# Where three adds and eight bias loads are issued: VectorE adds the gate's squares, ScalarE issues the attention's bias tiles

## The chip, the cores and the metric

The kernel runs on one core of one Trainium2 chip. The metric is the device time of an execution in microseconds (us). Engines are named as in the profile: PE is TensorE's matmul stream and PEld its weight loads, DVE is VectorE, ACT is ScalarE, POOL is GpSimd, SP is SyncE, which here only issues DMAs.

## The reference, cut to what matters

One step of a one-layer hybrid decoder, for a prompt of 512 tokens and for 8 samples of 4 new tokens each, with the same weights (all in fp32):

```
x += 0.5 * SwiGLU_1(RMSNorm(x))
h  = RMSNorm(x);  [q|k|v|u] = h @ W_in
x += concat(RMSNorm(DilatedAttn(q,k,v)), RMSNorm(S5_GLU(u))) @ W_out
x += 0.5 * SwiGLU_2(RMSNorm(x))
x += sigmoid(RMSNorm(x) @ W_gate) * (p @ W_ple);  final RMSNorm
```

DilatedAttn has 8 heads of 64 and three branches, (window 128, dilation 1), (512, 4) and (2048, 16), with a relative-position bias; the branches are merged by their log-sums. The samples attend to a cache of 2048 positions per sample, and the cache, shifted by four tokens, is an output as well. S5_GLU is a state-space scan, then `out = z * sigmoid(z @ w_glu + b_glu)` with z a GELU. The two places of the change lie in the RMSNorm of `out` (its sum of squares over 512 features) and in the prompt's bias, which is added to its scores.

## The kernel before, in words

Activations lie with features on the 128 partitions and all 544 tokens (512 prompt, 32 sample) along the free dimension. Every large weight is read from memory as a 128x512 `raw` tile, cast by ACT to a high part (`whi`, L175), and DVE subtracts to get the low part (`wlo`, L176); PE then does three matmuls per tile pair (L194). SP issues these weight loads from three `raw` buffers, and the large cache copies as well.

There are three stages. The first is the first feed-forward block (with the setup of the S5 tables beside it), until about 470 us. The second, mixed stage, holds the projections, the S5 half, the sample attention, the prompt attention and most of the output projection, until about 770 us. The third is the second feed-forward block and the gated embedding. In the first and the third stage the order of the instructions of PE, DVE, ACT and POOL is set by a planner at compile time, by its own timeline; SP's order is as written. In the mixed stage all five engines run in the order in which the Python code emits them, and that is written out by hand: `ORDER` is a list of step names, and every name advances one generator by one step (`do`, with what must have come before it in `need`).

The steps that matter here:

- `glu(m)`, four tiles. ACT makes the sigmoid, DVE multiplies (L1220), and `ssm_st.add(sg)` adds up the squares: the first call squares into the accumulator (L251), each later call has ACT square into a temporary tile (L254) and an adder engine add it (L255). Adders come from the list that `Stat` was made with. Then `split_gain` has ACT make `xh` (L299) and DVE `xl` (L300). The finished sum is read by PE at L263.
- `att_q`, 16 units of prompt scores (four head pairs of four row blocks). For each unit PE makes the scores (L1014), DVE adds the bias tile `bt` and takes the minimum (L1020), ACT takes the exponential (L1022) and scales by the reciprocal of the sum (L1025). `load_bt(hp)` loads the two bias tiles of a head pair, 128x512 each, from a table in memory; it is called once ahead of unit 0 and then at the end of the last unit of a head pair (units 3, 7, 11), for the next one. The tiles share a pool of eight slots with `L`, `pt`, `kb1` and `kt1`.
- `sample_scores` (names SQ) loads `kk` and `qb` through POOL's queue and multiplies them on DVE (L1099, L1100).
- `sample_out(gr)`, for two groups of four samples: nine accumulation steps on PE (L1191), each with a pair of V-cache tiles `vv` of 512 KB, which POOL issues one step ahead (L1178). `vv` shares six slots with `pz` (one per group) and with the tiles of the S5 half.

POOL's queue in the mixed stage thus holds, in the written order: loads of `kk`, `qb`, `kb1`, `bt` and `vv`, one store of `qD`, and the three adds of the GLU tiles.

Of the kernel before, what the change touches and what calls it, by code (L numbers as in the profile page):

```python
# [18 lines left out]
P = 128  # L19
# [9 lines left out]
DA = 512  # L29
# [73 lines left out]
def decoder_step(ctx: ExitStack, tc: tile.TileContext, a: dict, o: list):  # L103
    nc = tc.nc
    V, A, PE, SP, Q = nc.vector, nc.scalar, nc.tensor, nc.sync, nc.gpsimd

    def dram(t, off, dims):
        return bass.AP(tensor=t.tensor, offset=t.offset + off, ap=dims)
# [6 lines left out]
    def sb(pool, shape, name, dt=F32, **kw):  # L115
        return pool.tile(shape, dt, name=name, **kw)

    qD = dpool.tile([NS, DA], F32, name="qD")
    btD = dpool.tile([NH, P, 641], F32, name="btD")
# [622 lines left out]
    with ExitStack() as st:  # L742
# [255 lines left out]
        bts, Ls, pts = {}, {}, {}  # L998

        def load_bt(hp):  # L1000
            for e in range(2):
                bts[hp, e] = s5([P, 512], "bt")
                Q.dma_start(bts[hp, e], dram(btD, (2 * hp + e) * P * 641 + 127, [[640, P], [1, 512]]))

        def att_q():
            load_bt(0)
            yield
            for u, (hp, i) in enumerate(units):
                w = (i + 1) * P
                pss, mns = [], []  # L1010
                for e in range(2):
                    pr = slice(64 * e, 64 * e + 64)
                    ps = psm()
                    PE.matmul(ps[:, :w], qT[pr, hp, i * P:(i + 1) * P], kT[pr, hp, 0:w], start=True, stop=True)  # L1014
                    pss.append(ps)
                for e in range(2):
                    Ls[u, e] = L = s5([P, 512], "L")
                    mn = sb(small, [P, 4], "mn", bufs=4)
                    mns.append(mn)
                    V.tensor_tensor_reduce(L[:, :w], pss[e][:, :w], bts[hp, e][:, 512 - w:], -1.0, 3e38, ALU.add,  # L1020
                                           ALU.min, mn[:, 0:1])
                    A.activation(L[:, :w], L[:, :w], AF.Exp, scale=-1.0, bias=mn[:, 0:1], accum_out=mn[:, 1:2])  # L1022
                for e in range(2):
                    V.reciprocal(mns[e][:, 2:3], mns[e][:, 1:2])
                    A.activation(Ls[u, e][:, :w], Ls[u, e][:, :w], AF.Copy, scale=mns[e][:, 2:3])  # L1025
                if i == 3 and hp < 3:
                    load_bt(hp + 1)
                yield
# [174 lines left out]
            V.tensor_copy(att[:, :, S + 16 * gr:S + 16 * gr + 16], pf)  # L1203
            yield

        ssm_st, att_st = Stat(DA, (Q,)), Stat(DA)
        att_st.accs.append(sb(small, [P, NT], "sacc", bufs=2))
        att_sq = att_st.accs[0][:, :S]
        rs = {1: ssm_st, 0: att_st}
# [247 lines left out]
def run_tile(nc, args, outs):  # L1457
    with tile.TileContext(nc, schedule_with_timeline_sim=TS) as tc:
        with tc.manual_schedule(engines=ENG):
            decoder_step(tc, args, outs)  # L1460
# [18 lines left out]
```

## Time and profile before

| | |
|---|---|
| median of 3 runs | 1298.36 us (1295.39 to 1302.9) |
| the profiled execution | 1290.02 us, its span 1288.2 us |
| granted clock of PE, mean | 0.968 |
| PE matmul / PEld busy | 1208.3 us (94%) / 1142.4 us (89%) |
| DVE / ACT / POOL busy | 713.5 us (55%) / 446.1 us (35%) / 121.8 us (9%) |
| DMA | 231.30 MB, 180 GB/s in the mean |

How to read it: shares are of the span. An engine executes its instructions in order; a row of a timeline gives the start in us from the start of the span, the duration in us, the engine, the line, the operation with its tiles (output first) and, in brackets, how long the engine had been idle just before and what ended that. Instructions of one engine overlap a little, so a next start can lie before the end of the one ahead. PE's busy time is modelled, and a granted clock of 1.00 is TensorE's upper level.

### The profile page before, as it was taken

Reading aid. Unit: us, or ns where it says so; the run is one execution under the profiler, and the core shown is the slowest. Engines: PE = TensorE matmul, PEld = TensorE weight load, DVE = VectorE, ACT = ScalarE, POOL = GpSimd, SP = SyncE. Lnnn points to the kernel's source line nnn. Section 1 sums busy time; section 2 is a strip of 40 time slices with the busy share of each in tenths; the row PEclk is TensorE's granted clock in tenths of the full one; section 3 lists DMA queues with packets and bytes.
Section 4 is the critical chain, followed back from the end, with each engine's and each line's share of the span. In section 5 each row is a group of like instructions: output and inputs, shape, how many; then the busy total and the mean of one; then the engine's idle time right before and its main releaser. Section 6 shows DMA issues by size and latency. Waiting matters only on the chain.

```text
span 1288.2 us, 23223 instructions
## 1 busy us (share of the span) xinstructions
PE 1208.3 (94%) x9518; PEld 1142.4 (89%) x9518; DVE 713.5 (55%) x1499; ACT 446.1 (35%) x889; POOL 121.8 (9%) x195
## 2 busy tenths in 40 slices
PE   8999999999999999994769889999999999999995
PEld 7899999999999988983645449999999999999994
DVE  5544478476447638777775548444433444444455
ACT  5333322322233323121754445333322223333344
POOL 2200000233000112110123311000000000000000
PEclk8999999999999998996979989999999999999998
DMA  8484566668546549766358855445566455222321
GB/s 248 134 260 147 173 217 226 227 198 258 191 167 207 170 138 299 233 203 218 91 207 243 255 172 191 155 144 199 174 217 231 153 192 180 80 83 77 93 64 70
DMA packets 207547, 231.30 MB, mean 180 GB/s; under 512 B 8647, under 2 KB 187735, under 8 KB 206416
## 3 DMA queue, kind: packets, MB, share of 16 engines
q1 hardware_dynamic: 189552, 170.35, 40.8%
q0 software_dynamic: 17856, 59.45, 14.3%
q8 instruction: 75, 1.23, 0.4%
q14 instruction: 32, 0.26, 0.1%
q10 hardware_dynamic: 32, 0.01, 0.0%
HBM read 217.46 MB, written 81.89 MB: 232 GB/s over the span
## 4 chain that ended last, share of the span: by engine, by line
PE 81%; DMA 6%; DVE 5%; issue 4%; ACT 3%; POOL 1%; SPq 0%; ACTq 0%; POOLq 0%; DVEq 0%
PE acc L194 72%; DMA vv<-in_cache_v_dram 2%; DMA raw<-in_w_in_dram 1%; PE acc L206 1%; PE acc L1441 1%; DVE kk L1099 1%; DMA raw<-in_ffn_w_up_dram 1%; DMA pc<-pD 1%; PE sm L915 1%; PE po L1191 1%; DMA mm<-mD 1%; PE sm L910 1%; PE sm L263 1%; POOL vv L1178 1%; ACT L L1022 1%
## 5 line engine op out<-in xcount | busy, mean ns | idle before, releaser
L194 PE MATMUL acc<-xh,whi 128*128 128x272 f32 x1888 | 398.5, 292 | 5.9 <-DVE qT L773 1.3
L194 PE MATMUL acc<-xl,whi 128*128 128x272 f32 x1888 | 393.9, 290 | 0.7 <-DVE xl L304 0.3
L194 PE MATMUL acc<-xh,wlo 128*128 128x272 f32 x1888 | 393.4, 289 | 0.9 <-DVE wlo L176 0.9
L175 ACT CAST whi<-raw 128x512 fp32r<-128x512 f32 (+2 forms) x348 | 208.3, 606 | 531.1 <-PE acc L194 462.0
L176 DVE TENSOR_TENSOR wlo<-raw,whi 128x512 fp32r<-128x512 f32 (+2 forms) x348 | 231.1, 671 | 200.7 <-ACT whi L175 198.2
L194 PEld LDWEIGHTS acc<-xh,whi 128*128 128x128 f32 x1888 | 297.4, 189 | 12.0 <-issue 4.0
L194 PEld LDWEIGHTS acc<-xl,whi 128*128 128x128 f32 x1888 | 299.0, 190 | 1.9 <-DVE xl L304 0.8
L194 PEld LDWEIGHTS acc<-xh,wlo 128*128 128x128 f32 x1888 | 297.7, 189 | 1.4 <-DVE wlo L176 1.3
L194 PE MATMUL acc<-hh,whi 128*128 128x272 f32 x704 | 145.7, 288 | 0.0
L194 PE MATMUL acc<-hh,wlo 128*128 128x272 f32 x704 | 145.3, 288 | 0.0
L194 PE MATMUL acc<-hl,whi 128*128 128x272 f32 x704 | 145.2, 288 | 0.0
L194 PEld LDWEIGHTS acc<-hh,whi 128*128 128x128 f32 x704 | 110.7, 188 | 0.0
L194 PEld LDWEIGHTS acc<-hh,wlo 128*128 128x128 f32 x704 | 110.7, 188 | 0.0
L194 PEld LDWEIGHTS acc<-hl,whi 128*128 128x128 f32 x704 | 110.5, 188 | 0.0
L362 DVE TENSOR_TENSOR s<-acc,rstd 128x544 f32<-128x544 f32 x44 | 31.9, 724 | 87.3 <-PE acc L194 87.3
L356 DVE TENSOR_TENSOR s<-acc,rstd 128x544 f32<-128x544 f32 x44 | 31.9, 724 | 72.1 <-PE acc L194 65.9
L303 ACT CAST hh<-s 128x544 fp32r<-128x544 f32 x44 | 28.5, 647 | 78.9 <-DVE s L363 78.9
L304 DVE TENSOR_TENSOR hl<-s,hh 128x544 fp32r<-128x544 f32 x44 | 31.9, 725 | 27.3 <-ACT hh L303 27.3
L370 DVE SCALAR_TENSOR_TENSOR x<-acc,x 128x544 f32<-128x544 f32 x32 | 23.2, 725 | 36.0 <-PE acc L194 36.0
L1099 DVE TENSOR_TENSOR kk<-kk,qb 128x1024 f32<-128x1024 f32 x32 | 38.9, 1217 | 5.6 <-DMA qb<-qD 5.6
L1100 DVE TENSOR_REDUCE sc<-kk 128x16 f32<-128x1024 f32 x32 | 39.0, 1220 | 1.1
L357 ACT ACTIVATE s<-s 128x544 f32<-128x544 f32 x44 | 29.0, 659 | 11.5 <-DVE s L356 11.2
(397 smaller groups left out, 1116.6 us busy)
## 6 DMA issues: line engine op xcount, KB each, us to landing
out_dram<-in_cache_k_dram SPq DMA_DIRECT2D x32, 1022.0 KB, 7.0
out_dram<-in_cache_v_dram SPq DMA_DIRECT2D x32, 1022.0 KB, 6.0
raw<-in_ffn_w_gate_dram SPq DMA_DIRECT2D x44, 512.0 KB, 4.0
raw<-in_ffn_w_up_dram SPq DMA_DIRECT2D x44, 512.0 KB, 4.0
vv<-in_cache_v_dram POOLq DMA_DIRECT2D x36, 512.0 KB, 6.4
raw<-in_ffn_w_down_dram SPq DMA_DIRECT2D x32, 512.0 KB, 3.8
kk<-in_cache_k_dram POOLq DMA_DIRECT2D x32, 512.0 KB, 5.8
raw<-in_w_in_dram SPq DMA_DIRECT2D x16, 512.0 KB, 8.8
```

Source lines behind the costliest of these rows:

```text
L175: A.copy(hi[:, :len(p), :], r)
L176: V.tensor_tensor(lo[:, :len(p), :], r, hi[:, :len(p), :].bitcast(F32), ALU.subtract)
L194: PE.matmul(ps[:, h, :HT], wt[:, j, :], z[:, h * HT:(h + 1) * HT], start=done == 0 and n == 0, stop=done == len(ks) - 1 and n == 2)
L206: PE.matmul(ps[:, h, :HT], wt[:, j, :], z[:, h * HT:(h + 1) * HT], start=hf == 0 and j == 0 and n == 0, stop=hf == 1 and j == 3 and n == 2)
L303: A.copy(hi, src)
L304: V.tensor_tensor(lo, src, hi.bitcast(F32), ALU.subtract)
L356: V.tensor_tensor(v2(g1), pg[:, :, :HT], v2(rstd()), ALU.mult)
L357: A.activation(g1, g1, AF.Silu)
L362: V.tensor_tensor(v2(u1), pu[:, :, :HT], v2(rstd()), ALU.mult)
L370: V.scalar_tensor_tensor(v2(x[:, m, :]), ps[:, :, :HT], 0.5, v2(x[:, m, :]), ALU.mult, ALU.add)
L1099: V.tensor_tensor(t_, t_, qbs[n // 2], ALU.mult)
L1100: V.tensor_reduce(scs[b // 4][:, f, b % 4, 16 * jp:16 * jp + 16], t_.rearrange("p f (h d) -> p (f h) d", d=HD), AX.X, ALU.add)
```

## The change

Two lines. `Stat` is made without a list of adders for the gate's statistics, and its default is DVE alone; and the bias loads are issued from ACT's queue in place of POOL's.

```diff
         def load_bt(hp):
             for e in range(2):
                 bts[hp, e] = s5([P, 512], "bt")
-                Q.dma_start(bts[hp, e], dram(btD, (2 * hp + e) * P * 641 + 127, [[640, P], [1, 512]]))
+                A.dma_start(bts[hp, e], dram(btD, (2 * hp + e) * P * 641 + 127, [[640, P], [1, 512]]))
...
-        ssm_st, att_st = Stat(DA, (Q,)), Stat(DA)
+        ssm_st, att_st = Stat(DA), Stat(DA)
```

`Q` is POOL, `A` is ACT, `V` is DVE. The places of both in the written order stay the same. POOL keeps its part of the sums of the first norm and of the norm ahead of the second feed-forward block (`Stat(D, (Q, V))`).

## Rows read from the trace of the kernel before

**Rows 1.** The page's chain of waits: shares of the span by engine.
```profile
PE 81%; DMA 6%; DVE 5%; issue 4%; ACT 3%; POOL 1%; SPq 0%; ACTq 0%; POOLq 0%; DVEq 0%
```
**Rows 2.** Windows: length; busy of PE, PEld, DVE, ACT, POOL; PEclk; DMA share; GB/s.
```profile
640.00:690.00 50.00, 37.61 (x274) 28.04 (x275) 38.39 (x98) 30.06 (x73) 12.54 (x21) 0.83 0.60 195
690.00:725.00 35.00, 30.78 (x217) 16.91 (x217) 19.16 (x46) 13.44 (x35) 10.76 (x16) 1.00 0.90 265
...
880.00:1200.00 320.00, 320.00 (x2553) 319.81 (x2553) 134.20 (x205) 96.02 (x158) 0.00 (x0) 1.00 0.47 155
```
**Rows 3.** PE's waits, 640 to 690, then 690 to 775: us, times, longest.
```profile
PE pw L965 <- DVE mn L1020: 7.1, 2, 7.0
...
PE po L1191 <- DMA vv<-in_cache_v_dram: 6.1, 4, 2.7
```
**Rows 4.** Line 255, all its DVE instructions: ns min/median/max, first and last start.
```profile
L255 DVE TENSOR_TENSOR sacc<-sacc,s x20: 707/725/1874, 23.0 to 1203.2; 128x544 f32<-128x544 f32 x20
```
**Rows 5.** Line 300, its four instructions on s (the GLU tiles).
```profile
L300 DVE SCALAR_TENSOR_TENSOR xl<-s,gains,xh x4: 784/1370/1409, 630.4 to 655.6; 128x544 fp32r<-128x544 f32 x4
```
**Rows 6.** Timeline of DVE at the end of GLU tile 1.
```profile
634.67 1.35 DVE L300 SCALAR_TENSOR_TENSOR xl<-s,gains,xh 128x544 fp32r<-128x544 f32 x1 [1.37 <-ACT xh L299]
```
**Rows 7.** Timeline of ACT at the end of GLU tile 1.
```profile
633.34 0.66 ACT L254 ACTIVATE s<-s 128x544 f32<-128x544 f32 x1 [1.32 <-DVE s L1220]
633.90 0.73 ACT L299 ACTIVATE xh<-s,gains 128x544 fp32r<-128x544 f32 x1
```
**Rows 8.** Timeline of POOL, 634 to 728.
```profile
634.08 1.35 POOL L255 TENSOR_TENSOR sacc<-sacc,s 128x544 f32<-128x544 f32 x1 [13.84 <-ACT s L254]
...
663.65 1.46 POOL L1178 DMA_DIRECT2D vv<-in_cache_v_dram  x2
684.35 1.16 POOL L1003 DMA_DIRECT2D bt<-btD  x2 [19.25 <-DVE mn L1020]
685.51 2.13 POOL L1178 DMA_DIRECT2D vv<-in_cache_v_dram  x3
689.09 1.42 POOL L1178 DMA_DIRECT2D vv<-in_cache_v_dram  x2 [1.45 <-PE po L1191]
...
724.00 1.09 POOL L1003 DMA_DIRECT2D bt<-btD  x2 [2.67 <-ACT pt L1050]
725.08 2.13 POOL L1178 DMA_DIRECT2D vv<-in_cache_v_dram  x3
```
**Rows 9.** Timeline of PE: the S5 half's last transposes, then three waits for vv.
```profile
621.48 0.72 PE L928 MATMUL sm<-ident,ys 72*128 72x72 f32 x8 [0.51 <-ACT ys L918]
...
695.08 1.05 PE L1191 MATMUL po<-vv,pz 128*32 128x512 f32 x4 [0.55 <-DMA vv<-in_cache_v_dram]
698.02 1.05 PE L1191 MATMUL po<-vv,pz 128*32 128x512 f32 x4 [1.89 <-DMA vv<-in_cache_v_dram]
...
738.28 1.05 PE L1191 MATMUL po<-vv,pz 128*32 128x512 f32 x4 [2.66 <-DMA vv<-in_cache_v_dram]
```
**Rows 10.** The page's DMA issues: count, KB each, median us to landing.
```profile
vv<-in_cache_v_dram POOLq DMA_DIRECT2D x36, 512.0 KB, 6.4
...
raw<-in_w_in_dram SPq DMA_DIRECT2D x16, 512.0 KB, 8.8
...
raw<-in_w_out_dram SPq DMA_DIRECT2D x16, 256.0 KB, 2.9
```
**Rows 11.** Tile gt, ACT's only DMA: ns min/median/max, start.
```profile
L685 ACTq DMA_DIRECT2D gt<-in_norm_ffn_dram x1: 428/428/428, 0.7 to 0.7; - x1
```
**Rows 12.** Tile bt: its eight issues (ns), and their landing.
```profile
L1003 POOL DMA_DIRECT2D bt<-btD x8: 538/548/552, 544.9 to 724.5; - x8
...
DMA to landing us min/median/max: 3.0/3.2/5.0
```
**Rows 13.** Timeline of ACT at the end of unit 11 and the start of unit 12.
```profile
732.61 1.32 ACT L1025 ACTIVATE L<-L,mn 128x512 f32<-128x512 f32 x2
...
740.12 0.40 ACT L1022 ACTIVATE L<-L,mn 128x128 f32<-128x128 f32 x1 [4.86 <-DVE mn L1020]
```

## The prediction

> **What bounds the kernel now.** I read the chain of waits first, then windows over the stages, then the waits of TensorE (PE) in the middle stage. PE is 81% of the chain [rows 1]. From 880 us on a window is solid: 320.00 of 320.00 us of matmul [rows 2]. So an edit is worth what it takes out of PE's idle time. Both edits touch the mixed stage only, and there PE does idle: it is busy for 37.6 of 50 us in 640 to 690 and for 30.8 of 35 in 690 to 725 [rows 2]. Sorted by releaser, this idle time has two large entries: 7.1 us for VectorE (DVE) ahead of the small score matmuls at L965, and 6.1 us in four waits for V-cache tiles at L1191 [rows 3]. The change touches a cause of each.
>
> The run behind the profile took 1290.0 us (span 1288.2); the median of the runs shown is 1298.4, 8.3 us more. I work the gain out in the profiled run and take it off the median.
>
> **Part A, three adds from GpSimd (POOL) to DVE.** The list of adders was POOL alone, and the first square is written into the accumulator without an add; so 3 adds move, those of GLU tiles 1 to 3, which take POOL about 1.35 us each [rows 8]. On DVE the same line has a median of 0.725 us [rows 4]: 3 x 0.725 = 2.2 us more work in a stretch in which PE waits for DVE.
>
> Two things stand against it. First, L300, which follows the add, takes 0.78 us at the least but 1.37 in the median of its four instructions on s and 1.41 at most [rows 5]; tile 1's starts at 634.67, while POOL's add of 634.08 runs until 635.43 [rows 6, 8]. Without an add on POOL I expect 0.78 again: some 0.60 us back, three times. Second, DVE idles 1.37 us ahead of that L300, since ScalarE (ACT) makes the square (0.66, done at 634.00) and then xh (0.73, done at 634.63) [rows 6, 7]. The add needs the square alone, so it runs beside the making of xh, from about 634.0 to 634.72, and L300 starts 0.05 us later than now. Per tile 0.05 - 0.60 = -0.55 us, three times: -1.65 us.
>
> Does that reach PE? PE's longest wait for DVE, 7.0 us [rows 3], stands behind tiles 1 and 2 in DVE's order; an earlier DVE makes it shorter by as much, and tile 3 comes right after it. Bounds: +2.2 (every add on the path, no relief) to -1.8 (adds hidden wholly, relief in full). I take -1.65, since the row that shows the idle time is that of the place itself.
>
> By the Trainium skill, SBUF — State Buffer, section on the port that DVE and GpSimd share, a DVE instruction with two SBUF inputs and a GpSimd instruction that reads SBUF exclude each other, the later one waiting until the first ends. L300 has two such inputs, and a full block would have lengthened tile 1's by 635.43 - 634.67 = 0.76, where the rows have about 0.6. By that rule part A would be 3 x (0.05 - 0.76) = -2.1.
>
> **Part B, eight bias loads leave POOL's queue.** POOL issues in program order. The pair of bt for head pair 2 stands behind unit 7 of the score loop and ahead of the V loads of sample step 1. It waits 19.25 us for DVE at L1020, until 684.35; three vv loads go out right behind it at 685.51, without a wait of their own [rows 8]. POOL had been free since 663.65 + 1.46 = 665.1 [rows 8]. Do these three need slots that are still busy at 665? The pool has six: one holds pz, two hold the first V pair, and the last reads of the work that used them before, the transposes of ys at L928, end at 622.2 [rows 9]. So without bt the three go out from 665.1 on, 20 us earlier. The fourth waits for PE to read the first pair, and stays at 689.09 on PE's scale [rows 8].
>
> Now PE's waits. They are 0.55 us at 695.08 and 1.89 at 698.02, for the two tiles of step 2 [rows 9]. The second of these tiles is the one issued at 689.09; it took until 698.0, 8.9 us, behind the three of 685.51, where a vv load has a median of 6.4 [rows 8 to 10]. With the three landed long before, 689.1 + 6.4 = 695.5 is about when PE gets to it. I count both waits: -2.4 us.
>
> In the second sample group the pair of bt for head pair 3 waits until 724.00, and three vv stand behind it at 725.08 [rows 8]. They come forward by 3.7 us at most (the 2.67 of the wait and the 1.09 of the pair). The tile that PE waits 2.66 us for, at 738.28 [rows 9], is the one behind them, freed by PE itself; with the three out of its way I count half of its wait, -1.2. The fourth wait is paced by PE's own freeing of slots: nothing. Part B: -3.6 us. Bounds: 0 (no tile lands earlier) to -6.1 (all four waits go).
>
> The DMA share in 690 to 725 is 0.90 [rows 2]. A rule that speaks against part B: by the Trainium skill, Trainium Kernel Development and Optimization, Key Constraints, DMAs of all issuing queues run on the same 16 DMA engines, and spreading them saves the issue time of a sequencer alone. By it part B would be 0 and the sum -1.25.
>
> **Part C, ACT issues the bias loads.** ACT has issued one DMA so far, gt, which took its queue 0.43 us [rows 11]; POOL needs 0.55 for a bt [rows 12]. The queue counts most, so I take 0.43: 8 x 0.43 = 3.4 us, in four pairs of 0.86. Could ACT also wait there for a slot, with its casts queued behind it? What pair 2 waited for on POOL was L1020 of unit 7, and ACT's own L1025 of unit 7, just ahead of the pair, comes after that. Pair 3 was through at 724.00, and ACT gets there at 732.61 + 1.32 = 733.9 [rows 8, 13]. So no wait for a slot. Behind pair 3 ACT copies two pt tiles and then idles 4.86 us until 740.12 [rows 13], which swallows 0.86. Behind the others the work that follows feeds PE sooner; I take +0.4 in all. Bounds: 0 to 8 x 0.55 = +4.4.
>
> A later bt can make DVE wait. Issued at 733.9 to 734.8, with a landing of 3.0 to 5.0 us [rows 12], pair 3 is there by 737 to 739.8; ACT's next softmax step starts at 740.12, behind DVE's read of bt [rows 13]. With PE 1 to 2 us earlier this becomes tight, but a block of matmuls stands between that unit's scores and its transposes: 0.
>
> **Sum.** -1.65 - 3.6 + 0.4 = -4.85 us: 1285.2 in the profiled run, 1293.5 against the median. I call less than 0.5% (6.5 us) no measurable change; the forecast lies inside it.
>
> **Rivals.**
> 1. The transfers are the limit: 1.5 MB issued earlier does not make the later tiles land earlier, and the waits move to other steps. For it: the share of 0.90. Against it: 0.60 in 640 to 690, where the moved loads go [rows 2]. Parts A and C alone, -1.25: 1297.1 us.
> 2. All waits for vv go, part A is whole and C is hidden: -6.1 - 1.8 = -7.9, 1290.5 us. For it: five slots are full before step 0, a head start of 1.5 MB, 5.7 us at the 265 GB/s of 690 to 725 [rows 2]. Against it: the last steps of a group follow each other fast on PE.
> 3. Slower: the earlier V loads run into the weight tiles of the output projection, which SyncE issues in the same stretch. Those land in 2.9 us; w_in tiles, which meet traffic, need 8.8 [rows 10]. It decides once such a tile comes after ACT would cast it. Each exposed tile then costs PE 8.8 - 2.9 = 5.9 us, and two of them, 11.8 - 4.85 = +6.95: 1305.3 us. Against it: three raw buffers, loaded well ahead.
>
> **Chances.** The forecast 0.47, with its own range 1290 to 1297 us; rival 1 0.24; rival 2 0.16; rival 3 0.08; 0.05 for another order of instructions outside the stage, where a planner sets it, either way. The range 1286 to 1302 holds the forecast and rivals 1 and 2 with some spread of a median (the runs before lie between 1295.4 and 1302.9) and leaves rival 3 out; the worst bounds together, +2.2 + 4.4, would be 1305. Faster by over 0.5%, below 1291.9: rival 2 and some two fifths of the forecast, 0.35. Slower, above 1304.9: rival 3 and part of the rest, 0.12. Within: 0.53.
>
> **What would show it.** Part A: L300 on s near 0.78 four times, adds of 0.73 on DVE ahead of three of them, PE's longest wait for DVE near 5.9. Part B: five vv loads in a row from about 663, the waits of 0.55 and 1.89 gone, the one of 2.66 near 1.4. Part C: pairs of about 0.9 on ACT's queue with no wait ahead of them. I am wrong if L300 stays near 1.4, if vv loads wait for slots at 665, if PE's waits for vv still sum to 6, or if a cast waits for a w_out tile.

## The result, and the profile after

The changed kernel takes 1306.16 us in the median of 20 runs (1296.12 to 1314.06), the kernel before 1297.69 us in 20 runs beside it (1293.63 to 1305.22). The ratio is 1.0067, with a 95% interval from 1.0046 to 1.0088: slower by 0.7%, some 8.7 us, where 4.85 us less were forecast. The profiled execution of the changed kernel took 1302.12 us (span 1300.3), that of the kernel before 1290.02 (span 1288.2). Of all executions in this document one, of the kernel that loads 8 columns a second time, took 2081.48 us at a granted clock of 0.707; it is left out of that kernel's median and ratio.

First the chain of waits by engine and the windows, which answer to [rows 1, 2]; the window from 530 to 640 us was not among the rows ahead, and stands here for both kernels.

```profile
PE 77%; issue 12%; DMA 5%; DVE 3%; POOL 1%; ACT 1%; SPq 0%; ACTq 0%; POOLq 0%; DVEq 0%
```

After:

```profile
530.00:640.00 110.00, 83.56 (x691) 72.33 (x689) 72.75 (x147) 32.72 (x66) 10.55 (x20) 0.83 0.62 202
640.00:690.00 50.00, 36.58 (x253) 28.31 (x252) 37.79 (x93) 30.08 (x70) 6.72 (x11) 0.80 0.51 170
690.00:725.00 35.00, 33.65 (x253) 21.43 (x251) 22.43 (x48) 15.66 (x42) 8.49 (x12) 1.00 0.76 202
880.00:1200.00 320.00, 320.00 (x2553) 319.81 (x2553) 136.06 (x206) 96.84 (x159) 0.00 (x0) 1.00 0.48 159
```

Before:

```profile
530.00:640.00 110.00, 86.26 (x730) 75.15 (x724) 79.21 (x155) 38.43 (x77) 13.00 (x22) 0.88 0.59 187
```

The late part is solid in both. The chain's 12% of "issue" (4% before) are not read as a loss: this chain runs back over GpSimd's queue, for example through its 13.43 us of waiting for VectorE ahead of the kk load at 578.20. The loss is in the mixed stage, and it begins ahead of the part that the prediction worked on: from 530 to 640 PE is busy 2.7 us less, at a lower granted clock (0.83 instead of 0.88), and ScalarE and VectorE get 6 us less done each.

To place it I use a landmark, VectorE's two copies at L886, one in each half of the state-space layer. They are the same instructions in both kernels, and only the order of loads around the first pair of bias tiles differs between them. The row of the kernel before, then that of the kernel after (name, count, durations in ns, first and last start):

```profile
L886 DVE COPY hfin<-H x2: 174/174/174, 552.2 to 604.6; 128x16 f32<-128x16 f32 x2
```

```profile
L886 DVE COPY hfin<-H x2: 174/174/175, 553.8 to 612.9; 128x16 f32<-128x16 f32 x2
```

From the first to the second it takes 52.4 us before and 59.1 after: 6.7 us are lost here, more than half of the 12.1 between the two spans. Of the rest 1.6 us lie ahead of the first L886, where the kernels differ at most in the first pair's loads, 1.8 between the second L886 and the end of the sample attention, and 2.0 behind that; these were not traced. The experiments below count this interval, since the start of the stretch itself lies anywhere from 552 to 562 us in profiles of kernels that differ up to there at most in the first pair's loads.

**What the first pair meets.** In the written order the first pair of bias tiles is loaded early, as the token "aq" of the mixed stage. On GpSimd it went out behind a kk load, at 544.87 us, as the last load of a burst:

```profile
544.87 0.54 POOL L1003 DMA_DIRECT2D bt<-btD  x1
545.64 0.54 POOL L1003 DMA_DIRECT2D bt<-btD  x1 [0.23 <-issue]
```

No other load is issued until 555.99 us, and from about 550 on the DMA engines have next to nothing to do, so the pair runs out into a gap (busy share of the DMA engines, before, over 545 to 557 us, in 40 slices of 0.3 us, in tenths):

```profile
DMA  9999998999999521000000000000001000000000
```

On ScalarE the same place of the program lies behind the two activations that make ys at L918, which wait for PE (timeline of ACT, after):

```profile
558.48 0.59 ACT L918 ACTIVATE ys<-sm 72x512 f32<-72x512 f32 x1 [4.11 <-PE sm L915]
558.53 0.86 ACTq L1003 DMA_DIRECT2D bt<-btD  x2
```

So the pair leaves at 558.53: 13.7 us later by the two profiles, and 12 us later if counted from the first L886 (7.3 us ahead of it before, 4.7 us behind it after). SyncE is then issuing a group that PE needs at once, om and mm, two tables of the state-space layer, and a tile of w_in (timeline of SP, after), and GpSimd adds qb and kk loads:

```profile
557.89 1.25 SPq L896 DMA_DIRECT2D om<-coD  x2
559.24 0.62 SPq L898 DMA_DIRECT2D mm<-mD  x1
559.91 0.49 SPq L166 DMA_DIRECT2D raw<-in_w_in_dram  x1
```

The busy share of the DMA engines over 557 to 573 us, in 40 slices of 0.4 us (tenths), before and then after:

```profile
DMA  2875996889999999999999999999999630000009
```

```profile
DMA  0000298987789999999999999999999999999951
```

Before, the burst is over at about 569.5 us; after, with 0.5 MB more in it, at about 573. PE's L910 waits for mm, the load ahead of which the pair has slipped in (timeline of PE, before and then after):

```profile
565.96 0.66 PE L910 MATMUL sm<-mm,UC 128*72 128x128 f32 x4 [2.00 <-DMA mm<-mD]
...
572.12 0.52 PE L194 MATMUL acc<-xh,whi 128*128 128x272 f32 x2
```

```profile
571.28 1.10 PE L910 MATMUL sm<-mm,UC 128*72 128x128 f32 x4 [5.73 <-DMA mm<-mD]
...
578.20 0.66 PE L915 MATMUL sm<-om,H 64*72 64x128 f32 x8
578.79 0.52 PE L194 MATMUL acc<-xh,whi 128*128 128x272 f32 x2
```

The wait is 3.7 us longer. The blocks that follow take 7.5 us instead of 6.2 up to the next L194, since PE starts them at the lower of its two clock levels and stays there longer: from 572 to 577.5 the granted clock of after is 0.50, in a window of its own. At that L194 PE is 5.1 us behind. The next loads then inherit the delay, since SyncE's load of tab, another such table, waits for L910 and the two w_glu loads stand behind it (timeline of SP, after; before they went at 571.63 and 572.05):

```profile
578.30 0.37 SPq L836 DMA_DIRECT2D tab<-tabD  x1
578.77 0.95 SPq L166 DMA_DIRECT2D raw<-in_w_glu_dram  x2
```

Between the end of the burst and these loads the DMA engines have nothing to do (busy share over 573 to 585 us, in 40 slices of 0.3 us):

```profile
DMA  0100000000000000000008537999999999999999
```

Then ScalarE's casts wait for both w_glu tiles (timeline of ACT, after; before, the waits were 2.44 and 0.18), with the copy of vt, which PE needs, behind them:

```profile
584.30 0.62 ACT L175 CAST whi<-raw 128x512 fp32r<-128x512 f32 x1 [3.95 <-DMA raw<-in_w_glu_dram]
588.26 0.62 ACT L175 CAST whi<-raw 128x512 fp32r<-128x512 f32 x1 [3.34 <-DMA raw<-in_w_glu_dram]
588.78 0.58 ACT L946 COPY vt<-sm 128x512 f32<-128x512 f32 x1
```

VectorE stands behind these casts as well, since it makes `wlo` from each (L176), and the two L886 are its instructions. Less VectorE's waits, the time between them is 40.2 to 40.5 us in every profile below; so the interval grows by what VectorE waits. Its waits for ScalarE's `whi` between the two L886 (us, times, longest; 552 to 606 us before, 553 to 614 us after):

```profile
DVE wlo L176 <- ACT whi L175: 9.3, 1, 9.3
```

```profile
DVE wlo L176 <- ACT whi L175: 17.6, 3, 10.3
```

The longest one, for the w_in tile out of the burst itself, grew by 1.0 us only. The other two, 4.03 and 3.26 us for the w_glu tiles, are new, and some 1.7 us of waits for PE at L863 and L864 went away. So most of the 6.7 us comes by way of the late w_glu loads, which the late mm held back.

**The parts that were looked at ahead.** Waits over 530 to 790 us, of PE, which answer to [rows 3], and of VectorE:

```profile
PE sm L910 <- DMA mm<-mD: 11.3, 3, 5.7
...
PE po L1191 <- DMA vv<-in_cache_v_dram: 4.6, 3, 2.6
```

```profile
DVE L L1020 <- DMA bt<-btD: 11.6, 4, 6.2
```

The waits for vv fell from 6.1 to 4.6 us. VectorE's waits for bias tiles are new, and so are most of PE's for mm (3.0 before). Of these 11.3 us, 5.7 are the wait shown above; 4.0 stand ahead of the second half's L910, at 605.03, where the kernel before waits for other things (5.2 us for a DMA at 589.07, 1.9 for VectorE at 597.16), so not all of the sum is lost time. The adds and the instruction behind them, against [rows 5, 6] (line 300 on s, then the timeline of DVE at GLU tile 1):

```profile
L300 DVE SCALAR_TENSOR_TENSOR xl<-s,gains,xh x4: 781/782/784, 640.0 to 664.4; 128x544 fp32r<-128x544 f32 x4
```

```profile
643.65 0.73 DVE L255 TENSOR_TENSOR sacc<-sacc,s 128x544 f32<-128x544 f32 x1 [0.73 <-ACT s L254]
644.29 0.78 DVE L300 SCALAR_TENSOR_TENSOR xl<-s,gains,xh 128x544 fp32r<-128x544 f32 x1
```

GpSimd's timeline, against [rows 8], and PE's three waits for vv, against [rows 9]:

```profile
668.55 3.55 POOL L1178 DMA_DIRECT2D vv<-in_cache_v_dram  x5 [0.17 <-issue]
```

```profile
715.22 1.05 PE L1191 MATMUL po<-vv,pz 128*32 128x512 f32 x4 [1.05 <-DMA vv<-in_cache_v_dram]
...
731.20 1.05 PE L1191 MATMUL po<-vv,pz 128*32 128x512 f32 x4 [0.87 <-DMA vv<-in_cache_v_dram]
...
747.56 1.27 PE L1191 MATMUL po<-vv,pz 128*32 128x512 f32 x4 [2.64 <-DMA vv<-in_cache_v_dram]
```

Five vv loads go out in a row. The waits of 0.55 and 1.89 us are gone; the one at 715.22 is new; the other two answer to waits of 1.05 (at 721.91, before) and 2.66, and are 0.87 and 2.64. Landing of the bias tiles, against [rows 12], and two of VectorE's waits for them:

```profile
DMA to landing us min/median/max: 2.9/5.2/7.5
```

```profile
679.18 0.29 DVE L1020 CUSTOM_DVE_ANT_0 L<-sm,bt 128x128 f32<-128x128 f32 x1 [2.68 <-DMA bt<-btD]
...
749.83 0.29 DVE L1020 CUSTOM_DVE_ANT_0 L<-sm,bt 128x128 f32<-128x128 f32 x1 [6.18 <-DMA bt<-btD]
```

### The profile page after: what moved, and what is told of

The parts are those of the page before. It is cut to its first block, busy times and chain, and to the rows that moved or that the text cites. A ratio compares the mean times of both kernels' runs of the same rounds, so it can differ in the third digit from the quotient of the medians.

```text
span 1300.3 us, 23215 instructions
## 1 busy us (share of the span) xinstructions
PE 1214.8 (93%) x9518; PEld 1147.9 (88%) x9518; DVE 713.6 (55%) x1502; ACT 446.5 (34%) x889; POOL 113.1 (9%) x184
## 4 chain that ended last, share of the span: by engine, by line
PE 77%; issue 12%; DMA 5%; DVE 3%; POOL 1%; ACT 1%; SPq 0%; ACTq 0%; POOLq 0%; DVEq 0%
PE acc L194 70%; DMA vv<-in_cache_v_dram 2%; DMA raw<-in_w_in_dram 1%; PE acc L206 1%; PE acc L1441 1%; DMA raw<-in_ffn_w_up_dram 1%; POOL kk L1073 1%; PE po L1191 1%; PE sm L263 1%; DVE wlo L176 1%; DVE kk L1099 0%; POOL vv L1178 0%; PE sm L275 0%; DMA qb<-qD 0%; PE sm L1398 0%
## 5 line engine op out<-in xcount | busy, mean ns | idle before, releaser
L194 PE MATMUL acc<-xh,whi 128*128 128x272 f32 x1888 | 398.9, 293 | 6.2 <-DVE qT L773 1.3
L194 PE MATMUL acc<-xl,whi 128*128 128x272 f32 x1888 | 394.6, 290 | 0.5 <-DVE xl L304 0.3
L194 PE MATMUL acc<-xh,wlo 128*128 128x272 f32 x1888 | 393.6, 289 | 0.9 <-DVE wlo L176 0.9
L176 DVE TENSOR_TENSOR wlo<-raw,whi 128x512 fp32r<-128x512 f32 (+2 forms) x348 | 230.9, 670 | 211.4 <-ACT whi L175 208.9
L194 PEld LDWEIGHTS acc<-xh,whi 128*128 128x128 f32 x1888 | 297.7, 190 | 12.2 <-issue 5.7
L194 PEld LDWEIGHTS acc<-xl,whi 128*128 128x128 f32 x1888 | 300.0, 190 | 1.7 <-DVE xl L304 0.8
L194 PEld LDWEIGHTS acc<-xh,wlo 128*128 128x128 f32 x1888 | 298.1, 189 | 1.4 <-DVE wlo L176 1.3
L194 PE MATMUL acc<-hh,whi 128*128 128x272 f32 x704 | 145.7, 288 | 0.0
L194 PE MATMUL acc<-hh,wlo 128*128 128x272 f32 x704 | 145.4, 288 | 0.0
L194 PE MATMUL acc<-hl,whi 128*128 128x272 f32 x704 | 145.3, 288 | 0.0
L194 PEld LDWEIGHTS acc<-hh,whi 128*128 128x128 f32 x704 | 110.7, 188 | 0.0
L194 PEld LDWEIGHTS acc<-hh,wlo 128*128 128x128 f32 x704 | 110.7, 188 | 0.0
L194 PEld LDWEIGHTS acc<-hl,whi 128*128 128x128 f32 x704 | 110.5, 188 | 0.0
```

What stands on the lines that cost most here:

```text
L176: V.tensor_tensor(lo[:, :len(p), :], r, hi[:, :len(p), :].bitcast(F32), ALU.subtract)
L194: PE.matmul(ps[:, h, :HT], wt[:, j, :], z[:, h * HT:(h + 1) * HT], start=done == 0 and n == 0, stop=done == len(ks) - 1 and n == 2)
```

## The experiments

The theory after the first comparison: the loss is the first pair of bias tiles, whose loads ScalarE's order moves into a burst of loads that PE waits for. Its rivals: the adds on VectorE; the three later pairs, whose tiles VectorE waits for; ScalarE's issuing as such, which takes its queue's time; and chance in the one profile. All medians and ratios are against the kernel before, run beside them: 1298.98 us (28 runs) for the first four; 1298.27 (29) for the first pair later, the first pair earlier and the first timing of the last kernel; 1298.66 (17) for the two second loads and the two repeats; 1298.55 (17) for the second timing of the last kernel.

**The adds alone** (bias loads stay on GpSimd):

```
-        ssm_st, att_st = Stat(DA, (Q,)), Stat(DA)
+        ssm_st, att_st = Stat(DA), Stat(DA)
```

> Theory: the adds on DVE are a small gain, and the loss comes from the first pair of bias loads, which ScalarE issues late and into a burst of transfers. With the adds alone moved: L300 on s at 0.78 four times, PE's wait at L965 about 0.9 us shorter, the time 1 to 2 us under before (ratio 0.999). Rival 'the adds load the engine that PE waits for': 3 to 6 us over before.

Measured: 1296.84 us (12 runs), ratio 0.9990 (0.9971 to 1.0010), interval between the two L886 52.1 us. The adds are not the loss.

**The bias loads alone** (the adds stay on GpSimd):

```
-                Q.dma_start(bts[hp, e], ...)
+                A.dma_start(bts[hp, e], ...)
```

> All eight bias loads on ScalarE, the adds left on GpSimd. Theory: the whole loss and a little more, 9 to 12 us over before; PE waits 4 us or more for mm near 570, and DVE waits about 10 us for bt in sum. Rival 'the adds': at most 3 us over before.

Measured: 1303.60 us (8 runs), ratio 1.0043 (1.0020 to 1.0066), interval 60.3 us. The loss comes with this part. It is smaller than the 9 to 12 us expected, and VectorE's waits for bias tiles are 3.9 us, not about 10.

**Only the first pair on ScalarE** (adds on GpSimd):

```
+                (Q if hp else A).dma_start(bts[hp, e], ...)
```

> Only the first pair of bias loads moves to ScalarE; the other three pairs and the adds stay as before. Theory: the pair goes out near 558 in place of 545, beside the loads of om, mm, w_in, qb and kk; PE's waits for mm grow from 3 to about 11 us, and 5 to 7 us of the loss are there with one pair of four. Rival 'every load that ScalarE issues costs it': a quarter of the loss, about 2 us.

Measured: 1305.23 us (9 runs), ratio 1.0050 (1.0031 to 1.0069), interval 59.3 us, PE's waits for mm 12.6 us, no wait for a bias tile. One pair alone costs what all four cost.

**The changed kernel with the first pair back on GpSimd:**

```
-                A.dma_start(bts[hp, e], ...)
+                (A if hp else Q).dma_start(bts[hp, e], ...)
```

> The changed kernel with its first pair of bias loads back on GpSimd. Theory: most of the loss goes; from 0 to 3 us over before, since the three later pairs still land late behind the V loads (DVE waits some 10 us for bt) and the V loads come 3 us earlier. Rival 'every load that ScalarE issues costs it': three quarters of the loss stay, 6 us or more.

Measured: 1296.21 us (12 runs), ratio 0.9984 (0.9963 to 1.0006), interval 52.4 us. The loss is gone, though VectorE still waits 8.4 us for the other pairs: in the time those waits don't show (0 to 3 us over before was expected).

**The first pair later, on GpSimd** (kernel before; only the order is changed):

```
- ... SA SA M E SQ SA aq E SQ SQ M SB ...
+ ... SA SA M E SQ SA E SQ SQ aq M SB ...
```

> The kernel before, all bias loads and the sums of squares still on GpSimd; only the place of the first pair of bias loads in the written order is later, so that GpSimd issues it about 560 us instead of 545 us, into the stretch in which SyncE's om, mm and w_in loads and GpSimd's own qb and kk loads go out. Theory (the first pair costs because it goes out late, into that burst, whichever engine issues it): a good part of the 7 us between the first and the second L886 comes back, interval 55 to 60 us instead of 52.4, PE's waits for mm over 5 us in 530 to 790, and the time 0.2 to 0.5% above before (1301 to 1305 us). Rival (it is ScalarE's queue as such that delays the loads of SyncE): interval 52 to 53 us and the time within 0.2% of before.

Measured: 1302.72 us (12 runs), ratio 1.0030 (1.0003 to 1.0057), interval 54.2 us, waits for mm 2.1 us. The time came out as the theory said, the place didn't. GpSimd issued the pair at 567.53 us, 3.1 us behind mm (564.42) and not ahead of it; so mm was on time, and the w_in tile behind it was late: ScalarE's cast waited 15.0 us for it (13.0 before), and PE 2.9 us for the cast. The rest of the loss lies after the second L886, from which it is 163.8 us to the last L1202, against 160.8 before; it was not traced.

**The first pair earlier, on ScalarE** (the changed kernel; ahead of the two L918):

```
- ... SA SA M E SQ SA aq E SQ SQ M SB ...
+ ... SA SA M E SQ aq SA E SQ SQ M SB ...
```

> The changed kernel, but with the first pair of bias loads one place earlier in the written order, so that ScalarE issues it ahead of the two L918 that wait for PE, about 551 us instead of 558.5 us. Theory (the in-order wait on ScalarE is what moved the issue into the burst): most of the 7 us is gone, interval between the first and the second L886 52 to 55 us, time 1296 to 1301 us. Rival (the cost comes with ScalarE as the issuer, wherever it stands): interval stays at 59 us and the time at 1303 to 1307 us.

Measured: 1300.51 us (12 runs), ratio 1.0010 (0.9990 to 1.0031), interval 54.9 us, waits for mm 3.5 us. The same engine issues the pair, 8 us ahead of om, and most of the loss is gone. So it is the time of the issue and not the issuer.

**The first pair loaded a second time, whole.** This tells bytes from issue: GpSimd loads it at its old place, and ScalarE loads it again, with the same contents, where the changed kernel does.

```
                 Q.dma_start(bts[hp, e], ...)
+                hp or A.dma_start(bts[hp, e][:, :512], ...)
```

(`hp or` leaves the added line to the first pair, hp 0, alone.)

> The kernel before, with GpSimd loading the first pair of bias tiles at its old place, and ScalarE loading the same two tiles a second time (2 x 256 KB, same contents) at the place where the changed kernel issues them, behind the two L918. Nothing needs the second load soon. Theory (the 512 KB put into the burst of om, mm, w_in, qb and kk loads about 558 us delay these): 3 to 8 us slower than before (1301 to 1306 us), interval between the first and the second L886 56 to 60 us, PE's waits for mm well over the 3.0 us of before. Rival (the cost comes from the first pair's absence at its old place, or from the early part of the program): no slower than before.

Measured: 1310.14 us (6 runs), ratio 1.0075 (1.0048 to 1.0102). That is slower than the 1301 to 1306 us expected: besides the interval, 3.8 us more than before go after the second L886, which was not traced. The interval is 60.4 us (row of L886, then PE's wait), and mm lands 12.4 us after its issue:

```profile
L886 DVE COPY hfin<-H x2: 174/174/175, 560.6 to 621.0; 128x16 f32<-128x16 f32 x2
```

```profile
PE sm L910 <- DMA mm<-mD: 9.0, 3, 6.2
```

**The first pair loaded a second time, 8 of 512 columns:** the same edit with `[:, :8]`.

> As with the second load of the whole first pair, but ScalarE's second load brings only 8 of the 512 columns of each tile (2 x 4 KB): the same two issues in the same place of ScalarE's program, next to no bytes. Theory (bytes in the burst): within 0.2% of before (1296 to 1300 us), interval 52 to 54 us. Rival (ScalarE's two issues, 0.86 us each, hold up what stands behind them on ScalarE, or its queue as such costs): as slow as with the whole second load, 1301 to 1306 us, interval 56 us or more.

Measured: 1299.12 us (11 runs), ratio 0.9992 (0.9965 to 1.0018). The interval is 51.3 us, and mm lands 8.0 us after its issue:

```profile
L886 DVE COPY hfin<-H x2: 175/175/175, 557.7 to 609.0; 128x16 f32<-128x16 f32 x2
```

```profile
PE sm L910 <- DMA mm<-mD: 4.3, 2, 2.5
```

The two kernels have the same issues in the same places of ScalarE's program, and differ in 2 x 252 KB. That settles it: the bytes in the burst cost, the issuing doesn't. (ScalarE's two issues take 0.75 us together here, and 0.86 in the changed kernel, not 0.86 each.)

**The kernel before, once more,** unchanged, for a second profile:

> The kernel before, once more, for a second profile: the profiles so far fall into two groups by how early they reach the first L886 (552 to 554 us, or 559 to 562 us), with the time lost about 500 us, where no edit of these kernels stands. Theory: whichever group it falls in, the interval between the first and the second L886 is 52 to 54 us. Rival (the interval is a matter of chance, and 52.4 us was luck): 57 us or more.

Measured: 1293.63 us (1 run). It reaches the first L886 at 555.5 us, between the two groups, and the interval is 52.4 us again:

```profile
L886 DVE COPY hfin<-H x2: 174/174/175, 555.5 to 607.9; 128x16 f32<-128x16 f32 x2
```

**The first pair alone on ScalarE, once more,** unchanged:

> The first pair alone on ScalarE, once more, for a second profile. Theory: the interval between the first and the second L886 is again 57 to 60 us, and PE's waits for mm are over 8 us. Rival (chance): 52 to 54 us and 3 to 4 us.

Measured: 1300.30 us (1 run). The wait for mm is there again; the interval, 55.3 us, is under what was expected:

```profile
L886 DVE COPY hfin<-H x2: 174/174/175, 558.9 to 614.2; 128x16 f32<-128x16 f32 x2
```

```profile
PE sm L910 <- DMA mm<-mD: 12.1, 2, 6.4
```

The two casts of w_glu waited 4.5 us in sum here, against 7.3 in the changed kernel: how far the delay is passed on differs from run to run. The first L886 came late in this profile; with the whole second load it came later still, and the interval was 60.4. So a late start does not explain it.

**A kernel from what was found:** the adds on VectorE, and of the bias pairs only the third, the one that stood between the vv loads, on ScalarE.

```
+                (A if hp == 2 else Q).dma_start(bts[hp, e], ...)
```

> The sums of squares are added by VectorE, and of the four pairs of bias loads only the third is issued by ScalarE; the first, second and fourth stay with GpSimd. Theory (only the pair that stands between GpSimd's vv loads while PE waits for them is worth moving; the others only meet waits of VectorE for bias tiles): 0.2 to 0.4% under before (1294 to 1296 us), the wait of PE for vv that was 0.55 and 1.89 us shorter, and next to no wait of VectorE at L1020. Rival (the later pairs cost nothing either, and the change of the sums is the only gain): as with the first pair alone kept on GpSimd, 0.1 to 0.2% under before, not to be told from it.

Measured: 1296.33 us (12 runs), ratio 0.9981 (0.9959 to 1.0002). VectorE waits for no bias tile, and PE's waits for vv are 4.4 us. Timed a second time:

> The sums of squares on VectorE and the third pair of bias loads alone on ScalarE, timed once more, since its first interval (0.9959 to 1.0002) just reaches no change. Theory: again 0.1 to 0.3% under before, 1294 to 1297 us. Rival: the first result was chance, and it lies at or over before.

Measured: 1295.27 us (12 runs), ratio 0.9977 (0.9955 to 1.0000). Each interval just reaches no change. If the two are taken as independent, their mean is 0.9979, with a half width of about 0.0022 / 1.41 = 0.0016: a gain of about 0.2%, 2.7 us. It beats the changed kernel by far and the kernel before by a little; that it is better than the adds alone (0.9990) is not shown by the times. From the second L886 to L1202 it takes 158.4 and 159.0 us, against 160.8 and 161.4 before and 160.0 with the adds alone.

All profiles side by side, in us. The second column is the interval between the two L886, the third goes from the second L886 to the last matmul of L1202, where the sample attention ends; the fourth is VectorE's waits for `whi` between the two L886, with their number; the others are waits from 530 to 790 us, for VectorE up to 800.

| kernel | L886 to L886 | L886 to L1202 | VectorE for whi | PE for mm | PE for vv | VectorE for bt |
|---|---|---|---|---|---|---|
| before | 52.4 | 160.8 | 9.3 (1) | 3.0 | 6.1 | 0 |
| before, second | 52.4 | 161.4 | 9.3 (1) | 4.4 | 6.5 | 0 |
| after | 59.1 | 162.6 | 17.6 (3) | 11.3 | 4.6 | 11.6 |
| adds alone | 52.1 | 160.0 | 9.0 (1) | 4.2 | 6.1 | 0 |
| bias loads alone | 60.3 | 163.0 | 18.7 (3) | 8.9 | 4.6 | 3.9 |
| first pair on ScalarE | 59.3 | 160.7 | 17.7 (3) | 12.6 | 5.8 | 0 |
| the same, second | 55.3 | 161.7 | 14.0 (3) | 12.1 | 6.6 | 0 |
| after, first pair on GpSimd | 52.4 | 161.3 | 9.3 (1) | 3.8 | 4.5 | 8.4 |
| first pair later, GpSimd | 54.2 | 163.8 | 11.3 (1) | 2.1 | 7.3 | 0 |
| first pair earlier, ScalarE | 54.9 | 163.2 | 10.5 (1) | 3.5 | 4.1 | 10.9 |
| second load, whole | 60.4 | 164.6 | 18.4 (3) | 9.0 | 7.8 | 0 |
| second load, 8 columns | 51.3 | 161.5 | 9.1 (1) | 4.3 | 6.0 | 0 |
| third pair on ScalarE | 54.0 | 158.4 | 10.6 (1) | 5.4 | 4.4 | 0 |
| the same, second | 51.8 | 159.0 | 9.0 (1) | 1.3 | 4.3 | 0 |

In all five profiles in which the whole pair goes out between om and mm, VectorE waits three times, 14.0 to 18.7 us in sum; in the other nine it waits once, 9.0 to 11.3 us.

## Why the prediction was wrong

**Part A was right in its mechanism and near in size.** L300 on s takes 0.78 us four times, and the add of 0.73 us stands in VectorE's idle time ahead of it. The relief is 1.37 - 0.78 = 0.59 us per tile. By the Trainium skill, SBUF — State Buffer, section SBUF: two separate sides, the later of the two is blocked until the first ends; by the rows that would be 0.76 us for tile 1, and 0.81 and 0.83 for the other two. The rows agree that L300 is held up, but by 0.57 to 0.63 us. From tile 1's product (L1220) to VectorE's next L1020 it takes 16.0 us in the three kernels with the adds on GpSimd that were read for it (before, bias loads alone, second load whole) and 15.1 in three with the adds on VectorE (after, adds alone, first pair on GpSimd): 0.9 us for two tiles, where 1.1 were forecast. In tile 2 the square comes later, and the add waits 1.09 us for it instead of 0.73. PE's longest wait at L965 fell from 7.0 to 6.5 us, not to the 5.9 that was named; that alone shows little, since it is 6.5 also in two kernels with the adds on GpSimd (bias loads alone, second load whole). Forecast -1.65 us; the adds alone measured 0.10% less, that is -1.3 us, with an interval from -3.8 to +1.3.

**Part B was right in its first group and wrong in its second.** The five loads in a row and the end of the two waits came as worked out. The 1.2 us in the second group did not: the wait of 2.66 us is 2.64, so the three loads ahead of that tile had not been what delayed it: the pair of loads that PE frees goes out at 741.08 us, and the wait ends 6.5 us later, as it did before (731.79 to 738.28). And one wait of 1.05 us came at a later step of the first group, the part of rival 1 (the waits move to other steps) that was true. The sum went from 6.1 to 4.6 us, -1.5 instead of -3.6. The stretch from the second L886 to L1202 is no shorter for it in the changed kernel (162.6 us against 160.8 and 161.4); it is where only the third pair moved (158.4 and 159.0).

**Part C failed, and with it the forecast.** The step that failed is "Behind the others the work that follows feeds PE sooner; I take +0.4 in all". It priced an issue by the time that it takes on ScalarE's queue, and that price was about right: 0.86 us for the first pair and 1.47 for the longest, 3.9 for all four where 3.4 were taken, and issuing alone (the second load of 8 columns) cost nothing. What was not asked for each pair is when ScalarE gets to it and what is then on the way. Head pairs 2 and 3 (the third and the fourth) were followed from row to row; the first pair, 544.9 in [rows 12] and far from the stage that the argument was about, was not. Its issue moved by 12 us, counted from the first L886, into the burst of om, mm and w_in, and that one pair cost 0.50% (0.31 to 0.69), some 6.5 us. With it back at its old place and all the rest of the change kept, the time is 0.16% under before (0.37 under to 0.06 over), 2.1 us: not clear of no change, and less than half of the 4.85 that were forecast.

**"A later bt can make DVE wait ... 0"** was wrong in the trace: 11.6 us in four waits, one of them 6.18 us at head pair 3, whose margin had been called tight. In the time it doesn't show: with three pairs on ScalarE the waits are 8.4 us, and the kernel is as fast, within its interval, as with one pair on ScalarE and no such wait (0.9984 against 0.9981 and 0.9977). That it is worth nothing is not shown: from the second L886 to L1202 the first takes 161.3 us in its one profile, the other 158.4 and 159.0.

**The rivals.** The third, slower because moved transfers collide with loads of SyncE, had the kind of mechanism and nearly the time (1305.3 against 1306.2 us), but the wrong transfers and the wrong place: it looked at the V loads and the output projection, and it was the bias tiles and the loads of the state-space layer. Its price was that of two tiles of w_out, so that the time came near is luck. It had 0.08, for it was argued from those loads that come earlier; the loads that come later were not weighed. The rule that was quoted against part B, by the Trainium skill, Trainium Kernel Development and Optimization, Key Constraints, that all issuing queues share the same 16 DMA engines, says the same from the other side, and the second loads agree with it: 512 KB on ScalarE's queue hold up loads on SyncE's, and 8 KB don't.

**What stays open.** At the 380 GB/s that the burst of the changed kernel moves from 561 to 571 us, the pair's 0.52 MB are 1.4 us, and mm came 3.7 us later (4.4 us later with the whole second load than with 8 columns, 12.4 against 8.0 us from issue to landing). In which order the 16 engines serve the queues was not measured. That PE's lower clock after the longer wait adds 1.3 us is read from one profile. Why the pair issued later by GpSimd, and the whole second load, also lose time after the second L886 was not traced.

## What to carry to other kernels

When an issue moves to another engine, write down for every DMA of it, not for those of one stage alone, the instruction that it now stands behind, the time at which it will leave, and the loads that leave beside it. The cost of the issue on the queue is the small part; 0.5 MB that nobody needs for 60 us, put in front of a load that TensorE is about to wait for, cost 6.5 us; issuing them took 0.86 us of ScalarE's queue, and issuing alone showed no cost. To tell the two apart, issue the same DMA in the same place with few bytes.

## What was not expected of the hardware

In the profiles of the two second loads, the landing time did not depend on the size. These loads, of 256 KB each and of 4 KB each, have the same median from issue to landing (DMA issues of 560 to 600 us, the whole load and then 8 columns):

```profile
bt<-btD ACTq DMA_DIRECT2D x2, 256.0 KB, 7.6
```

```profile
bt<-btD ACTq DMA_DIRECT2D x2, 4.0 KB, 7.6
```

So the landing time did not tell what the load cost others: mm, issued behind them, landed after 12.4 us in the first kernel and after 8.0 in the second.

The delay is also much larger than the transfer: a load that comes 3.7 us late holds PE at the lower clock for some blocks more, keeps the next loads from being issued while the DMA engines idle for over 5 us, and makes VectorE wait 7.3 us for what they bring; the interval grows by 6.7 us. And the same DMA takes ScalarE's queue between 0.33 and 1.14 us, against 0.54 to 0.55 on GpSimd [rows 12].
